# First products on x times its gain, with rstd applied to the results; pooling, head margins and adaptive-norm sums in another order

## The chip, the cores and the metric

One NeuronCore of a Trainium2 chip runs the whole program; nothing is shared with other cores. The metric is the device time of one execution in microseconds. Five engines work from queues of their own, each in order: TensorE (PE: products and transposes), VectorE (DVE), ScalarE (ACT), GpSimd (POOL) and SyncE (SP, which here only starts loads). They meet only through semaphores. POOL, ACT and SP can each start DMA loads; a load that must wait holds up everything behind it on the queue that starts it.

## The reference

256 tokens of width 2048 go through two transformer blocks. What matters here of the first is the norm, the first products and the two mixers:

```python
h = rms_norm(x, pre_mix_g)          # x * rstd * g, rstd one number per token
z = h @ w_in                        # q, k, v, u: 1024 columns each
a = chunked_attention(q, k, v, rel_bias)   # 8 heads of 128, chunks of 64 tokens
p = multiscale_pool(u, pool_w, pool_scale) # trailing means over 2, 4, 8, 16 tokens, minus the token
m = concatenate([a, p]) @ w_o
x = x + rms_norm(m, post_mix_g)
# then an FFN with gelu and a depthwise convolution over tokens, D_FF = 5632
```

The second block has adaptive norms: silu(c) @ w_ada + b_ada gives shifts, scales and gates for the token stream, and the same with c_ctx for a context of 256 tokens. w_ada has 2048 x 12288 numbers. The shift and scale of the first norm are needed before the second block's first product, the gates and the second norm's pair later. The block's k and v are computed for context and tokens together, then come 24 heads, gates, an output product and a second FFN.

## The kernel before

**Products.** All weights are float32. Every weight piece (128 x 1024, 512 KB) is loaded by SP into one of 4 buffers w, then split: ACT rounds it to h (L237, `prep`), DVE computes l = w - h (L238). Activations are kept as such a pair too. A product is h.h + l.h + h.l, so PE multiplies three times. There are 5 pairs of h and l; `fill`, called after each step of a product (`done`), prepares pieces as long as buffers allow, so ACT and DVE run some four pieces ahead of PE. `token_major` (L392, L393, L395) gives results with tokens on partitions: one block of 128 rows of weights is 6 matmuls of 512 columns for two token tiles, 12 for four. `feature_major` (L359) gives 128 features with 256 tokens on columns, in four steps of 8 matmuls; `folded` (L367 on ACT, L368 on DVE) adds its two halves and frees the bank.

**Order.** Code order is the order on every engine. `Side` holds generators of side work (pools, heads, norms of the second block): after each step of a product a `tick` advances one of them, or two in later stages, up to its next `yield n`, which lets n ticks pass. `side.until` ticks until a condition holds, with no product in between.

**Start.** SP loads x for the first 128 tokens, the gain row broadcast to all partitions (prg, 1 MB), four weight pieces, then x for the other tokens (L608, L610, L204). Per token tile: squares on ACT (L477), their sum and rsqrt (L426, L428 on DVE, a power on POOL, L429), x * rstd * g on DVE (L439), transposes on PE (L452), split into the pair (L337, L338). The first product, half of v, runs on 8 blocks for tile 0 alone, then makes tile 1, then goes on with both (`staged`). After it the conditioning rows are loaded (cc), passed through silu and written to DRAM (crow), to come back as broadcast rows (`ada_rows`, L510).

**After it.** vout splits v (L337, L338). DVE zeroes part of the probabilities' tiles by copying the zero margin of ut (L654), which POOL sets (L652) after another memset, on the table of position biases (tab, loaded as rb, L651). Then q and k are projected, heads 0 to 3 are added as side work, u is projected, and after every second feature block a `pool` is added: POOL adds shifted copies (L666), DVE scales and subtracts (L669 to L673), ACT and DVE split (L675, L676).

**Sums for w_ada.** Products with one row are done on DVE: tiles of w_ada come on POOL's queue into two buffers v (L211), one DVE instruction multiplies with the broadcast row and accumulates (L536). The first 64 tiles (shift and scale, both streams) take two sums each, every later tile one. `pace`, a number of sums per step from the table PACE (its first entry for feature_major, its second for token_major), spreads them over the products: entry 0 up to the first FFN, 1 in it, 2 in the second block's k and v, then two more. `limit` is the count of tiles allowed so far, `hold` the tick before which none may run. The rows for the sums and the gain of the last norm of block 1 (pfg) share one buffer, adat.

**Second block's k and v.** Six chunks of 512 columns for four token tiles (context and tokens). Seven banks hold results, so a chunk starts with three free banks and waits for the fourth: square on ACT (L1158), sums per head (L1159), power on POOL (L1161), scaling from the bank on DVE (L1190). Results go to DRAM on POOL's queue (L1196).

Of the kernel before, what the change touches and what calls it, by code (L numbers as in the profile page):

```python
# [20 lines left out]
F32 = mybir.dt.float32  # L21
# [14 lines left out]
PACE = ((0.3, 0.35), (0.19, 0.33), (0.0, 0.88), (0.0, 0.3), (0.1, 0.13))  # L36
# [154 lines left out]
class Stream:  # L191
# [10 lines left out]
    def load(self):  # L202
        while self.loaded < len(self.items) and self.loaded < self.mains + len(self.w):
            self.nc.sync.dma_start(self.w[self.loaded % len(self.w)], self.items[self.loaded])  # L204
            self.loaded += 1
# [65 lines left out]
class Kernel:  # L271
# [216 lines left out]
    def constants(self):  # L488
# [12 lines left out]
        self.small = self.g(P)  # L501
# [95 lines left out]
    def block1(self):  # L597
# [5 lines left out]
        xr = a["x"].rearrange("(t p) d -> p t d", p=P)  # L603
        nc.scalar.copy(self.stats[:, 0:1], self.mhalf)
        grow = self.slot(4, F32)[:, :D]
        for t in range(2):
            for c in range(4):
                nc.sync.dma_start(xt[:, t, c * 512:(c + 1) * 512], xr[:, t, c * 512:(c + 1) * 512])  # L608
            if t == 0:
                nc.sync.dma_start(grow, a["prg"].to_broadcast([P, D]))  # L610
                S.load()
        nc.scalar.dma_start(self.vecs, a["vec"])
        self.xs = self.ring(512, 4)

        def start(t):
            ss = self.stat(4)
            for c in range(4):
                self.sumsq(xt[:, t, c * 512:(c + 1) * 512], ss[:, c:c + 1])
            return self.pre_norm(t, xt, ss, grow)
        self.meet(self.norm_b(start(0), 0, hh, hl))  # L620
        xs1 = start(1)
        first = self.token_major([(hh, hl, 0), (hh, hl, 1)], self.staged(lambda: self.norm_t(xs1, 1, hh, hl)))
        cc = self.small[:32]
        nc.gpsimd.dma_start(cc, a["cc"])
        nc.scalar.activation(cc, cc, AF.Silu)
        nc.gpsimd.dma_start(self.crow.rearrange("o (j p) -> (o j) p", p=P), cc)
        self.pace = PACE[0]
        self.ada_begin({0: 0, 1: 2}, 64)
# [8 lines left out]
        scr = [s6[:, 2048 + i * 384:2048 + (i + 1) * 384] for i in range(4)]  # L637
        self.gtop = self.gbase + 1024 + 2048
# [9 lines left out]
        self.half = half  # L648
        nc.gpsimd.dma_start(tab, a["rb"])
        nc.gpsimd.dma_start(inv, a["inv"])  # L650
        nc.gpsimd.memset(tab[0:64, :, 192:256], NEG)  # L651
        nc.gpsimd.memset(ut[:, :, :16], 0.0)  # L652
        for i in range(4):
            nc.vector.tensor_copy(pt[:, i % 2, i // 2, 1, :P], ut[:, :8, :16])  # L654

        def pool(g):

            w = 2 ** (g + 1)
# [3 lines left out]
            while step < w:  # L662
# [4 lines left out]
                cur, step = dst, 2 * step  # L667
            fix = self.stat(32).rearrange("p (k t) -> p k t", k=2)
# [49 lines left out]
        def head(h):  # L718
# [10 lines left out]
            sc = 1.0 / math.sqrt(P)  # L729
            mx, sm = self.stat(2), self.stat(2)  # L730
            for q, (lo, hi) in enumerate(((0, P), (P, 384))):
                nc.vector.scalar_tensor_tensor(s[:, lo:hi], bank[:, 2 * lo:2 * lo + hi - lo], sc, tab[:, h, P:] if q == 0 else tab[:, h, :],
# [33 lines left out]
        vout(first)  # L766
        qkproj(0)
# [148 lines left out]
    def ffn1(self, pair, x, mid):  # L916
# [58 lines left out]
        def chunk_end(gi, c, t, bank):  # L975
# [11 lines left out]
            if gi == len(GROUPS) - 2 and c == 3 and t == 1:  # L987
                side.drain()
                S.finish()
# [590 lines left out]
```

## Time and profile before

| | |
|---|---|
| Median of 3 runs | 2774.2 us (2769.51 to 2774.95) |
| The profiled execution's own time | 2776.85 us |
| Its span, first to last instruction | 2775.1 us |
| Busy: PE, DVE, ACT, POOL | 97%, 73%, 48%, 9% |
| Mean granted clock of PE | 0.993 of 2.4 GHz |
| DMA | 608.91 MB, mean 219 GB/s |

PE is busy nearly all the time, so the shares say little on a change that leaves PE's work as it is. What PE waits for is read from the stages: 0 to 41 us is the start and the first product, 41 to about 320 the mixers of block 1, 320 to 368 the norms before the first FFN, 368 to 1058 that FFN, 1138 to 1404 the second block's k and v. The columns of a timeline row are start, duration, engine, line, operation, output and input, and in brackets the idle time before it and what ended it.

### The profile page before, as it was taken

To read this page: it belongs to the slowest core of one execution; us is meant where nothing else is said; L and a number is where in the kernel's file an instruction comes from. 1 tells how busy PE (TensorE), PEld (TensorE's weight loads), DVE (VectorE), ACT (ScalarE), POOL (GpSimd) and SP (SyncE) were. 2 spreads that over 40 slices of the span, in tenths; PEclk is the share of its full clock that TensorE was granted. 3 is DMA by queue.
4 is the path that set the end of the run, shared out by engine and by line. 5 is a ranking of instruction groups with operands and counts; after the bars stand their busy time and mean duration, and the time that the engine had idled before them with its cause. 6 is when DMAs were issued, how large, how long until landed. Compare 5 with 4: busy or idle time off the path is not lost.

```text
span 2775.1 us, 36806 instructions
## 1 busy us (share of the span) xinstructions
PE 2699.4 (97%) x13654; PEld 2274.2 (82%) x13654; DVE 2015.8 (73%) x2938; ACT 1336.8 (48%) x1994; POOL 248.8 (9%) x395
## 2 busy tenths in 40 slices
PE   7989899999999999998999999999999999999999
PEld 6878788888888887777777788888878888888887
DVE  5878787888887767767577877778766666665566
ACT  5444455545455645321256655644454444444443
POOL 1010000000000000222211100011000000000000
PEclk9999999999999999999999999999999999999999
DMA  7666667676776765666855544489857777766565
GB/s 264 199 217 230 241 211 259 220 251 215 244 238 207 227 191 168 232 245 243 292 178 178 171 155 156 148 322 322 274 170 227 236 230 233 234 198 195 185 205 166
DMA packets 167573, 608.91 MB, mean 219 GB/s; under 512 B 19472, under 2 KB 19664, under 8 KB 166368
## 3 DMA queue, kind: packets, MB, share of 16 engines
q1 hardware_dynamic: 127728, 461.43, 49.6%
q0 software_dynamic: 39520, 144.87, 15.8%
q8 instruction: 107, 1.75, 0.3%
q14 instruction: 74, 0.61, 0.1%
q10 hardware_dynamic: 144, 0.25, 0.0%
HBM read 591.76 MB, written 14.71 MB: 219 GB/s over the span
## 4 chain that ended last, share of the span: by engine, by line
PE 78%; DVE 3%; DMA 3%; ACT 2%; issue 2%; POOL 0%; DVEq 0%; ACTq 0%; POOLq 0%
PE bank L359 34%; PE bank L392 14%; PE bank L393 13%; PE bank L395 13%; DMA v<-wada 3%; PE bank L342 1%; DVE l L238 1%; PE bank L343 1%; PE bank L344 1%; PE bank L1275 1%; ACT h L237 1%; DMA G<-kv 0%; ACT G L477 0%; PE bank L452 0%; DVE G L536 0%
## 5 line engine op out<-in xcount | busy, mean ns | idle before, releaser
L238 DVE TENSOR_TENSOR l<-w,h 128x1024 fp32r<-128x1024 f32 x870 | 1059.9, 1225 | 357.6 <-ACT h L237 346.8
L237 ACT CAST h<-w 128x1024 fp32r<-128x1024 f32 x870 | 908.9, 1051 | 615.8 <-PE bank L393 430.9
L359 PE MATMUL bank<-pair,h 128*128 128x512 f32 x3072 | 842.8, 395 | 6.5 <-DVE slot L338 3.5
L359 PEld LDWEIGHTS bank<-pair,h 128*128 128x128 f32 x3072 | 526.7, 189 | 76.4 <-issue 3.7
L392 PE MATMUL bank<-h,pair 128*128 128x512 f32 x1344 | 539.3, 401 | 24.1 <-DVE slot L1190 10.3
L393 PE MATMUL bank<-h,pair 128*128 128x512 f32 x1344 | 530.0, 394 | 2.1 <-DVE G L426 1.4
L359 PEld LDWEIGHTS bank<-pair,l 128*128 128x128 f32 x3072 | 470.1, 189 | 66.6 <-DVE l L238 0.8
L359 PE MATMUL bank<-pair,l 128*128 128x256 f32 x3072 | 488.1, 281 | 0.1
L395 PE MATMUL bank<-l,pair 128*128 128x512 f32 x1344 | 416.0, 395 | 6.0 <-DVE l L238 5.9
L536 DVE CUSTOM_DVE_ANT_0 G<-v,G 128x1024 bf16<-128x1024 f32 x256 | 327.8, 1280 | 70.5 <-DMA v<-wada 68.8
L392 PEld LDWEIGHTS bank<-h,pair 128*128 128x128 f32 x1344 | 256.5, 191 | 83.5 <-issue 16.3
L395 PEld LDWEIGHTS bank<-l,pair 128*128 128x128 f32 x1344 | 255.3, 190 | 64.0 <-DVE l L238 9.5
L393 PEld LDWEIGHTS bank<-h,pair 128*128 128x128 f32 x1344 | 256.3, 191 | 53.6 <-DVE G L426 1.8
L392 PE MATMUL bank<-h,slot 128*128 128x512 f32 x768 | 299.1, 390 | 1.0 <-ACT slot L337 1.0
L393 PE MATMUL bank<-h,slot 128*128 128x512 f32 x768 | 299.0, 389 | 0.0
L395 PE MATMUL bank<-l,slot 128*128 128x512 f32 x768 | 237.7, 389 | 0.0
L211 POOL DMA_DIRECT2D v<-wada x192 | 102.1, 532 | 1337.7 <-DVE G L536 1281.0
L367 ACT COPY G<-bank 128x256 f32<-128x256 f32 x192 | 71.6, 373 | 278.5 <-PE bank L359 278.2
L392 PEld LDWEIGHTS bank<-h,slot 128*128 128x128 f32 x768 | 144.2, 188 | 30.8 <-ACT slot L337 1.5
L393 PEld LDWEIGHTS bank<-h,slot 128*128 128x128 f32 x768 | 144.2, 188 | 30.4 <-DVE slot L338 0.5
L395 PEld LDWEIGHTS bank<-l,slot 128*128 128x128 f32 x768 | 144.1, 188 | 30.0
L368 DVE TENSOR_TENSOR G<-bank,G 128x256 f32<-128x256 f32 x192 | 81.1, 422 | 109.4 <-ACT G L367 109.1
(217 smaller groups left out, 1700.4 us busy)
## 6 DMA issues: line engine op xcount, KB each, us to landing
v<-wada POOLq DMA_DIRECT2D x192, 512.0 KB, 4.8
w<-wup SPq DMA_DIRECT2D x176, 512.0 KB, 4.3
w<-wgu SPq DMA_DIRECT2D x176, 512.0 KB, 4.0
w<-wdn SPq DMA_DIRECT2D x88, 512.0 KB, 4.5
w<-wfd SPq DMA_DIRECT2D x88, 512.0 KB, 4.1
w<-w SPq DMA_DIRECT2D x66, 512.0 KB, 4.5
w<-w2g SPq DMA_DIRECT2D x64, 512.0 KB, 3.5
w<-w2kv SPq DMA_DIRECT2D x52, 512.0 KB, 4.4
```

What stands on the lines that cost most here:

```text
L211: self.nc.gpsimd.dma_start(t, src)
L237: self.nc.scalar.copy(h, w)
L238: self.nc.vector.tensor_sub(l, w, h.bitcast(F32))
L342: t.matmul(out, ah, bh, start=start, stop=False)
L343: t.matmul(out, ah, bl, start=False, stop=False)
L359: t.matmul(bank[:, :size], w[:, j * P:(j + 1) * P], x[:, kb, :size], start=s == n == 0, stop=s == 3 and n == 7)
L367: self.nc.scalar.copy(z, bank[:, 256:])
L368: self.nc.vector.tensor_add(out, bank[:, :256], z)
L392: self.nc.tensor.matmul(banks[i], xh, h, start=seen[i] == 1, stop=False)
L393: self.nc.tensor.matmul(banks[i], xl, h, start=False, stop=False)
L395: self.nc.tensor.matmul(banks[i], xh, l, start=False, stop=seen[i] == total[i])
L536: nc.vector.tensor_tensor_reduce(out=self.junk.bitcast(mybir.dt.bfloat16), in0=w, in1=self.adat[:, slot * 1024:(slot + 1) * 1024], scale=1 ...
```

## The change

The first norm is taken apart. x is multiplied by g alone, in chunks of 512 columns, transposed and split; rstd comes later and is applied to the product's results: to v while it is split (L809, L810 of the new kernel), to u and k by an extra DVE multiplication with a row rt of rstd per token (L741, L731), to q through the heads' scale (rq in place of the constant). The row rt goes through DRAM: two writes of 128 numbers (rrow) and one broadcast load. x and the gain are loaded chunk by chunk on three queues, with weight pieces between them on SP. The first product does one block, then chunk 1 is made, four blocks, chunk 2, four blocks, chunk 3, and the rest. Silu, crow and the table's memset become side work (`side_rows`). A pool starts after the one before and yields between POOL's adds and DVE's part. The sums get other paces, and when the first 64 tiles are done in the first FFN, 24 tiles more are allowed there, before the second block.

```diff
-PACE = ((0.3, 0.35), (0.19, 0.33), (0.0, 0.88), (0.0, 0.3), (0.1, 0.13))
+PACE = ((0.2, 0.3), (0.24, 0.36), None, (0.0, 0.3), (0.1, 0.13))
...
+        if kind == 0:
+            self.ada_begin({0: 0, 1: 1}, 88)
...
+        for c in range(4):
+            (nc.scalar if c == 0 else nc.gpsimd).dma_start(grow[:, cs[c]], a["prg"][:, cs[c]].to_broadcast([P, 512]))
+            nc.sync.dma_start(xt[:, 0, cs[c]], xr[:, 0, cs[c]])
+            if c < 2:
+                S.load(2 * c + 1)
+            (nc.scalar if c == 0 else nc.gpsimd).dma_start(xt[:, 1, cs[c]], xr[:, 1, cs[c]])
+            if c < 2:
+                S.load(2 * c + 2)
...
+        def scaled(c, t):
+            z, bank = xs(), self.sb()
+            nc.vector.tensor_mul(z, xt[:, t, cs[c]], grow[:, cs[c]])
+            for j in range(4):
+                nc.tensor.transpose(bank[:, j * P:(j + 1) * P], z[:, j * P:(j + 1) * P], self.ident)
+            return bank
...
+        first = self.token_major([(hh, hl, 0), (hh, hl, 1)], [
+            self.seg(range(1), after=lambda: chunk(1)), self.seg(range(1, 5), after=lambda: chunk(2)),
+            self.seg(range(5, 9), after=lambda: chunk(3)), self.seg(range(9, KB))])
+        for c in (2, 3):
+            squares(c)
+        rrow = self.dpool.tile([1, 256], F32, name="rrow")
+        for t in range(2):
+            self.rstd(ss[t], D, rr[:, t:t + 1], count=4)
+            nc.gpsimd.dma_start(rrow[:, t * P:(t + 1) * P].rearrange("o p -> p o"), rr[:, t:t + 1])
+        nc.vector.tensor_scalar_mul(rq, rr, 1.0 / math.sqrt(P))
...
+        nc.gpsimd.dma_start(rt, rrow.to_broadcast([P, 256]))
...
+        nc.gpsimd.memset(ut[:, :, :16], 0.0)
         nc.gpsimd.dma_start(tab, a["rb"])
         nc.gpsimd.dma_start(inv, a["inv"])
-        nc.gpsimd.memset(tab[0:64, :, 192:256], NEG)
-        nc.gpsimd.memset(ut[:, :, :16], 0.0)
...
         def pool(g):
 
+            while g and g - 1 not in pool_done:
+                yield 1
...
+            yield 2 + g
             fix = self.stat(32).rearrange("p (k t) -> p k t", k=2)
...
-                self.folded(self.feature_major(hx), ut[:, fb, 16:])
+                u = self.folded(self.feature_major(hx), ut[:, fb, 16:])
+                nc.vector.tensor_mul(u, u, rt)
...
+                    if which:
+                        nc.vector.tensor_mul(last, last, rt)
...
-                self.split(vt[:, 0, t, :], vt[:, 1, t, :], banks[t])
+                v, r = vt[:, 0, t, :], rr[:, t:t + 1]
+                nc.scalar.activation(v, banks[t], AF.Identity, scale=r)
+                nc.vector.scalar_tensor_tensor(vt[:, 1, t, :], banks[t], r, v.bitcast(F32), op0=ALU.mult, op1=ALU.subtract)
...
-                self.pace = PACE[2]
+                self.pace = 0.0, (132 - S.vdone) / 80
```

On DVE at the very start, the old kernel begins with the statistics of the first token tile (G) and goes over to pairs of l and pair:

```order
L426 TENSOR_REDUCE G<-G 128x1
L428 TENSOR_SCALAR G<-G 128x1
L439 SCALAR_TENSOR_TENSOR G<-slot_104,G,slot_107 128x512 x4
L238 TENSOR_TENSOR l_87<-w_78,h_82 128x1024
L338 TENSOR_TENSOR pair_105<-bank_75,pair_105 128x4x128
L238 TENSOR_TENSOR l_88<-w_79,h_83 128x1024
```

The new one begins with two multiplications of chunk 0 (slot_104 is x, slot_106 the gain):

```order
L625 TENSOR_TENSOR G<-slot_104,slot_106 128x512 x2
L239 TENSOR_TENSOR l_87<-w_78,h_82 128x1024
L339 TENSOR_TENSOR pair_105<-bank_75,pair_105 128x4x128
L239 TENSOR_TENSOR l_88<-w_79,h_83 128x1024
L339 TENSOR_TENSOR pair_105<-bank_76,pair_105 128x4x128
L239 TENSOR_TENSOR l_89<-w_80,h_84 128x1024
L239 TENSOR_TENSOR l_90<-w_81,h_85 128x1024
L625 TENSOR_TENSOR G<-slot_104,slot_106 128x512 x2
```

The statistics are gone from there, and the multiplications of chunk 1 stand behind the l of the fourth piece. On POOL, the old kernel has between the first rsqrt and the first w_ada tile (v):

```order
L429 TENSOR_TENSOR G<-G 128x1 x2
L624 DMA G<-cc 32x128
L626 DMA crow<-G 32x128
L510 DMA G<-crow 128x1024 x2
L649 DMA slot_332<-rb 128x2048
L650 DMA G<-inv 128x64
L651 MEMSET slot_332 64x8x64
L652 MEMSET G 128x8x16
```

and the new one, after six loads of x and the gain:

```order
L430 TENSOR_TENSOR G<-G 128x1
L654 DMA rrow<-G 128x1
L430 TENSOR_TENSOR G<-G 128x1
L654 DMA rrow<-G 128x1
L666 DMA slot_334<-rrow 128x256
L678 MEMSET G 128x8x16
L679 DMA slot_334<-rb 128x2048
L680 DMA G<-inv 128x64
L687 DMA G<-cc 32x128
L690 DMA crow<-G 32x128
L511 DMA G<-crow 128x1024 x2
L693 MEMSET slot_334 64x8x64
```

The zero margin (128x8x16) moved ahead of rb and behind rrow. In the norm of the context, which runs in the first FFN, POOL before has only the context's loads:

```order
L872 DMA G<-ctx 128x512 x4
L429 TENSOR_TENSOR G<-G 128x1
L879 DMA G<-ctx 128x512 x4
```

and now, at the same place:

```order
L920 DMA G<-ctx 128x512
L212 DMA v_93<-wada 128x1024
L430 TENSOR_TENSOR G<-G 128x1
L927 DMA G<-ctx 128x512
L212 DMA v_92<-wada 128x1024
L212 DMA v_93<-wada 128x1024
L212 DMA v_92<-wada 128x1024
L927 DMA G<-ctx 128x512
```

Tiles of w_ada now stand between them. Counted over DVE's list, the sums before the first FFN go from 55 to 41, those in it from 73 to 111, those in the second block's k and v from 64 to 40, and the later ones are 64 as before. Of those in the FFN, 24 stand between the fourth group's down product and the fifth group's up product, where before had none. PE has the same 8841 rows in both.

## Rows read from the trace of the kernel before

**Rows 1.** The page's busy line.
```profile
PE 2699.4 (97%) x13654; PEld 2274.2 (82%) x13654; DVE 2015.8 (73%) x2938; ACT 1336.8 (48%) x1994; POOL 248.8 (9%) x395
```
**Rows 2.** Stretches: from:to us, length, PE busy (count), PE clock, DMA share, GB/s.
```profile
0.00:41.00 41.00, 28.84 (x131) 1.00 0.76 275
41.00:62.00 21.00, 17.55 (x92) 0.92 0.65 237
...
130.00:172.00 42.00, 32.59 (x149) 0.92 0.43 137
...
368.00:1058.00 690.00, 690.00 (x3673) 1.00 0.69 226
...
1225.00:1264.00 39.00, 36.86 (x156) 0.96 0.57 207
1264.00:1302.00 38.00, 30.51 (x124) 0.87 0.61 220
```
**Rows 3.** Timeline of the start: us, duration, engine, line, operation.
```profile
9.94 2.74 DVE L439 SCALAR_TENSOR_TENSOR G<-slot,G,slot 128x512 f32<-128x512 f32 x4 [1.16 <-DMA slot<-prg]
...
11.11 1.05 ACT L237 CAST h<-w 128x1024 fp32r<-128x1024 f32 x1 [2.70 <-DMA w<-w]
...
12.60 1.22 DVE L238 TENSOR_TENSOR l<-w,h 128x1024 fp32r<-128x1024 f32 x1
...
21.68 2.64 PE L452 MATMUL bank<-G 128*128 128x128 f32 x16 [1.39 <-DVE G L439]
...
24.08 0.48 PE L392 MATMUL bank<-h,pair 128*128 128x512 f32 x1
...
40.50 1.07 ACT L337 CAST slot<-bank 128x512 fp32r<-128x512 f32 x2 [0.27 <-PE bank L395]
```
**Rows 4.** Start's stretches, all engines (PE, PEld, DVE, ACT, POOL); GB/s last.
```profile
0.00:8.00 8.00, 0.00 (x0) 0.00 (x0) 0.00 (x0) 3.95 (x9) 0.79 (x8) 1.00 0.72 244
8.00:16.00 8.00, 5.25 (x24) 4.86 (x25) 6.37 (x10) 5.30 (x9) 0.57 (x1) 1.00 1.02 406
```
**Rows 5.** Timeline around the first q projection.
```profile
53.26 0.52 POOL L651 MEMSET slot<- 64x512 f32 x1 [6.48 <-DMA slot<-rb]
...
53.95 0.63 DVE L654 CAST slot<-G 128x128 fp32r<-128x128 f32 x4 [14.09 <-POOL G L652]
...
55.33 2.04 PE L359 MATMUL bank<-pair,h 128*128 128x512 f32 x4 [3.45 <-DVE slot L338]
```
**Rows 6.** DMA issues from 39 to 56: KB each, us to landing.
```profile
crow<-G POOLq DMA_DIRECT2D x1, 16.0 KB, 3.8
```
**Rows 7.** Timeline around the third pool.
```profile
145.17 4.31 POOL L666 TENSOR_TENSOR G<-G 128x542 f32<-128x542 f32 x3 [4.76 <-DVE G L368]
...
149.51 0.19 DVE L669 TENSOR_TENSOR G<-G 128x32 f32<-128x32 f32 x1 [3.29 <-POOL G L666]
...
151.46 1.99 ACT L237 CAST h<-w 128x1024 fp32r<-128x1024 f32 x2
...
152.55 0.80 PE L392 MATMUL bank<-h,pair 128*128 128x512 f32 x1 [5.65 <-ACT h L237]
```
**Rows 8.** Page, costliest groups: multiplication-like DVE work on 256 columns.
```profile
L368 DVE TENSOR_TENSOR G<-bank,G 128x256 f32<-128x256 f32 x192 | 81.1, 422 | 109.4 <-ACT G L367 109.1
```
**Rows 9.** Page, costliest groups: the sums for w_ada.
```profile
L536 DVE CUSTOM_DVE_ANT_0 G<-v,G 128x1024 bf16<-128x1024 f32 x256 | 327.8, 1280 | 70.5 <-DMA v<-wada 68.8
```
**Rows 10.** DVE's waits from 1138 to 1380: total us, times, longest.
```profile
DVE G L536 <- DMA v<-wada: 64.0, 45, 3.6
```
**Rows 11.** PE's waits from 1374 to 1404.
```profile
PE bank L1264 <- DMA G<-kv: 3.8, 1, 3.8
PE bank L561 <- DVE G L536: 1.6, 1, 1.6
```
**Rows 12.** DVE busy in two stretches of the first FFN.
```profile
836.00:880.00 44.00, 31.06 (x43) 1.00 0.69 222
880.00:972.00 92.00, 69.78 (x115) 1.00 0.67 217
```

More of the change, by code (lines that the diff above doesn't have):

```diff
@@ L200, in __init__, with load @@
         self.pace, self.credit, self.limit, self.hold = 0.0, 0.0, 0, 0
-    def load(self):
-        while self.loaded < len(self.items) and self.loaded < self.mains + len(self.w):
+    def load(self, most=None):
+        most = len(self.items) if most is None else most
+        while self.loaded < most and self.loaded < self.mains + len(self.w):
             self.nc.sync.dma_start(self.w[self.loaded % len(self.w)], self.items[self.loaded])
@@ L500, in constants @@
         self.junk = self.g(512)
-        self.small = self.g(P)
+        self.small, self.rx = self.g(P), self.g(4)
         make_identity(nc, self.ident)
@@ L615, in start @@
[L615 to L625, printed above, removed]
@@ L626, in block1 @@
-        nc.gpsimd.dma_start(self.crow.rearrange("o (j p) -> (o j) p", p=P), cc)
-        self.pace = PACE[0]
-        self.ada_begin({0: 0, 1: 2}, 64)
+        grow = self.slot(4, F32)[:, :D]
+        cs = [slice(c * 512, (c + 1) * 512) for c in range(4)]
+        for c in range(4):
[6 more added lines that the diff above has]
+                S.load(2 * c + 2)
@@ new lines, in block1 @@
+        nc.scalar.dma_start(self.vecs, a["vec"])
+        nc.scalar.copy(self.stats[:, 0:1], self.mhalf)
+        xs = self.ring(512, 4)
+        ss = [self.ss[:, :4], self.ss[:, 4:]]
+        rq, rr = self.rx[:, :2], self.rx[:, 2:]
+        def scaled(c, t):
[4 more added lines that the diff above has]
+            return bank
@@ new lines, in parts, with chunk, squares @@
+        def parts(c, t, bank):
+            self.split(*(d[:, 4 * c:4 * c + 4, t * P:(t + 1) * P] for d in (hh, hl)), bank.rearrange("p (k t) -> p k t", k=4))
+        def chunk(c):
+            for t, bank in enumerate([scaled(c, 0), scaled(c, 1)]):
+                parts(c, t, bank)
+            if c > 1:
+                squares(c - 2)
+        def squares(c):
+            for t in range(2):
+                self.sumsq(xt[:, t, cs[c]], ss[t][:, c:c + 1])
+        begin = scaled(0, 0), scaled(0, 1)
@@ new lines, in block1 @@
+        for t in range(2):
+            S.prep()
+            parts(0, t, begin[t])
+        first = self.token_major([(hh, hl, 0), (hh, hl, 1)], [
[4 more added lines that the diff above has]
+        rrow = self.dpool.tile([1, 256], F32, name="rrow")
+        for t in range(2):
+            self.rstd(ss[t], D, rr[:, t:t + 1], count=4)
+            nc.gpsimd.dma_start(rrow[:, t * P:(t + 1) * P].rearrange("o p -> p o"), rr[:, t:t + 1])
@@ L648, in block1, with side_rows @@
         self.half = half
+        nc.gpsimd.memset(ut[:, :, :16], 0.0)
         nc.gpsimd.dma_start(tab, a["rb"])
         nc.gpsimd.dma_start(inv, a["inv"])
[L651 to L652 removed]
         for i in range(4):
             nc.vector.tensor_copy(pt[:, i % 2, i // 2, 1, :P], ut[:, :8, :16])
+        def side_rows():
+            cc = self.small[:32]
+            nc.gpsimd.dma_start(cc, a["cc"])
+            yield 6
+            nc.scalar.activation(cc, cc, AF.Silu)
+            nc.gpsimd.dma_start(self.crow.rearrange("o (j p) -> (o j) p", p=P), cc)
+            self.pace = PACE[0]
+            self.ada_begin({0: 0, 1: 2}, 64)
+            nc.gpsimd.memset(tab[0:64, :, 192:256], NEG)
+            yield 1
         def pool(g):
+            while g and g - 1 not in pool_done:
+                yield 1
             w = 2 ** (g + 1)
@@ L988, in chunk_end @@
                 side.drain()
+                S.limit = 64
                 S.finish()
                 side.drain()
-                assert S.vdone == 64 and len(self.ada_done) == 8
+                S.limit = S.vdone
+                assert len(self.ada_done) == 8
                 for n in range(4):
```

13 lines of the change are left out of this document (3 added, 10 removed).

## The prediction

> **What bounds the kernel now.** I read the page's busy line first: TensorE (PE) is busy 97% of the span [rows 1]. Then the table of stretches for PE [rows 2], cut where the program changes. The reader is to see two things there: from 368 to 1058 us (the first FFN) PE has no idle time at all, and what it loses elsewhere lies in a few short stretches. I count a stretch's loss as its length minus PE's busy time, plus its length times (1 - granted clock), since each of the lower figures comes from pieces at 1.2 instead of 2.4 GHz. That gives 12.2 us for 0 to 41; 3.5 + 1.7 = 5.1 for 41 to 62; 9.4 + 3.4 = 12.8 for 130 to 172; 2.1 + 1.6 = 3.7 for 1225 to 1264; 7.5 + 4.9 = 12.4 for 1264 to 1302. The order lists hold the same 8841 rows on PE in both kernels, so PE's own work is unchanged and the change can only give or take waits and clock. The rest is therefore: which wait of PE ends later or sooner, taken by stretch from the timelines and from the list of who waited for whom.
>
> **Start, 0 to 41 us.** Before, the first product ends at 40.50, when ScalarE (ACT) reads its bank; its last 72 matmuls start at 24.08, so one takes 0.228 us [rows 3]. The change splits x * g into chunks, and PE does one block of 6 matmuls, then the transposes of chunk 1, then the rest. On VectorE (DVE) the two multiplications of chunk 1 stand behind all of the first four l subtractions (the order list shows it), so they wait for the fourth weight piece. By then 4 pieces, 4 chunks of x and 2 of the gain must have come, 3.67 MB; with vec and all else on the ACT and POOL queues it is 4.97 MB. At the rates before, 244 and then 406 GB/s [rows 4], this is there at 12.2 or 15.4 us. Then come a cast of 1.05, a subtraction of 1.22, two multiplications of 0.69 (2.74 for 4 of their nearest kind) and a group of transposes of 0.66 (2.64 for 4 groups) [rows 3]: 4.3 us. PE then has 90 matmuls, 20.5 us, and 4 groups of transposes, 2.6 us. The product ends between 39.6 and 42.8, so -0.9 to +2.3 us. PE is idle for some 3 us in the middle of this. After waits of 3.5 and 5.7 us the clock fell [rows 2, 5, 7], and the shorter of these cost 1.7 us; that makes the upper end +4. I take +3, nearer that end, because three queues send at once and nothing puts the four pieces first. The statistics and the wait for the rsqrt, which stood ahead of the multiplication, go; but DVE was held there by the gain's load anyway, and the weights are late next.
>
> No row before shows three queues loading together. The Trainium skill, "DMA: Bandwidth & Descriptors", section "Issuing engines are not separate DMA queues", says that loads issued on several engines run on the same 16 DMA engines and interleave, and that spreading them saves only issue time. By that rule the later chunks on POOL delay the pieces, and the start is at or above the upper end just given; with full precedence for the pieces it would be at the lower.
>
> **First q projection, 41 to 62.** PE waited 3.5 us for DVE, whose copies (L654) waited for a POOL memset that stood behind another memset, which waited for the 1024 KB load of rb until 53.26 [rows 5]. Now the memset of the margin stands ahead of that load, but behind the two writes of rrow and the load that waits for them. A 16 KB write of this kind took 3.8 us [rows 6]; with some 4 us (an estimate) for the last squares, two reductions, two powers and two issues ahead of it, the memset runs about 8 us after the product ends. PE first missed DVE at 55.33 - 3.5 = 51.8, 11.3 us after the product's end. Two copies' and subtractions' time lies between, so about 1 us is left and the stall goes: -5.1, or -1 if the element-wise rrow write takes 4 us more. I take -5.
>
> **Pools and heads, 62 to 320.** In 130 to 172 PE's longest wait (5.7 us) ends with an ACT cast of weights at 151.46; ahead of that cast on ACT stands the pool's cast, which waits for DVE, which waits for three POOL adds of 4.3 us together [rows 7]. So a side task blocked two in-order queues that feed PE. Now each pool waits for the one before and lets 2 to 5 ticks pass between its adds and DVE's part; a tick has about 1.4 us of PE work behind it (four matmuls of 0.228 and four of half the columns), so 2.7 to 6.8 us. The largest pool has four adds of about 1.4 us, 5.7 us, just inside its 6.8. All of it would be -12.8; if POOL's adds are late behind a w_ada load, which itself waits for a sum on DVE, perhaps -5. I take -11. The 16 added multiplications by rstd cost 16 x 0.42 = 6.7 us of DVE [rows 8], and 14 fewer sums before the FFN give back 14 x 1.28 = 17.9 [rows 9]; neither is on PE's path, as DVE has idle time there. vout, the heads' scale and the other replaced operations keep their kind and size: nothing.
>
> **Second block's k and v, 1138 to 1404.** DVE waited 64.0 us here for w_ada tiles, 45 times [rows 10]: with two buffers the sums run as fast as loads land, and DVE falls behind the weights. In the fourth chunk, PE then waits 7.5 us for the evacuation; in the third, with the same instructions, only 2.1 [rows 2]. The change leaves 40 sums instead of 64, at 44/80 = 0.55 per block instead of 0.88, so the fourth chunk should cost what the third costs: 12.4 - 3.7 = -8.7. The floor is 0, if the wait is the chain's own. At the end PE waited 1.6 us for the last sum and 3.8 for kv [rows 11]; the last sums now come with slack, and the kv stores no longer stand behind the gate row: -2, between 0 and -5.
>
> **First FFN, 368 to 1058.** The sums moved there are not free. By the order lists 24 of them fall between the fourth group's down product and the fifth group's up product (836 to 972), where before had none. DVE is busy 31.06 of 44 and 69.78 of 92 there [rows 12]; 24 x 1.28 = 30.7 makes it 131.5 of 136. The ctx loads now also stand between w_ada loads on POOL. PE's cover is the weight pieces prepared ahead (four, some 11 us of PE work). Between 0 and +12; I take +4. Elsewhere in this FFN 14 more sums are spread over 470 us, where PE never waited: nothing.
>
> **Sum.** +3 - 5 - 11 - 8.7 - 2 + 4 = -19.7. The profiled execution took 2776.85 us (span 2775.1), so 2757.15; the median shown, 2774.2, lies 2.65 below it, which gives 2754.5.
>
> **Rivals.**
> - *The start loses more.* The later chunks take their full share, the pieces come at the end of the 4.97 MB, landing adds about 1 us and two pieces of low clock cost 3.4: +6.7 instead of +3, 2758.2. For it: the multiplications stand behind the fourth piece. Against: the SP queue alone holds the weights, in larger rows than x. This is where the skill's rule above would put the time. Chance 0.17.
> - *The pools' wait only moves.* POOL's adds still wait for DVE through the w_ada loads between them, DVE still waits for POOL: -1 instead of -11, 2764.5. For it: POOL's list still has such loads between adds. Against: the yields. Chance 0.1.
> - *The change doesn't do what it says at the k and v chunks*: the 7.5 us are the square, reduction and power in a row, not the sums: 2763.2. Against: the third chunk has the same chain and waits 2.1. Chance 0.1.
> - *The first FFN becomes bound by DVE*, the slower side. If from 836 on each of the 24 sums also waits for its tile as in [rows 10] (64.0/45 = 1.4 us), DVE needs 131.5 + 34 = 165.5 for 136, and with the in-order waits for ACT that its busy time doesn't hold, some 15 us (an estimate), 180. PE loses what exceeds 136 + 11 = 147: 33 instead of 4, 2784. It decides from the point where DVE's need passes 147. Against: at 0.24 and 0.36 per block (1.4 us of PE) the sums come every 4 to 6 us there, and in the k and v chunks before every 3.1 (0.88 per 2.7 us). Chance 0.05.
> - *My forecast*: 0.55, with a range of its own of 2746 to 2761. The remaining 0.03 is better than it: all terms at their lower ends, 2740.
>
> The range 2744 to 2768 holds the forecast and the first three rivals and leaves out the slower one and the best ends. About 0.2% (5.5 us) is what a measurement of this kernel can tell from no change: slower than before + 0.2% is the FFN rival, less the part of it that comes out milder, 0.04; within 0.2% (above 2768.7) that part and two small rivals together, 0.06; faster 0.90.
>
> **What would show it.** Right: the first product ends near 43 us; PE's wait of 3.5 near 52 and of 5.7 near 147 are gone, and the clock's low pieces with them; DVE's waits for wada in the k and v chunks fall from 64 to under 15 us; the fourth chunk's wait is near 2. Wrong: DVE waits for POOL of more than 3 us before the FFN, an L359 or L392 wait on an l subtraction between 836 and 1058, or a product that ends after 46.

## The result: 46 us slower

The changed kernel takes 2820.95 us (median; 2819.85 to 2822.52), the kernel before beside it 2774.57: a ratio of 1.017 with a 95% interval of 1.0153 to 1.0188. The forecast was 2754.5 us. The profiled execution has a span of 2819.4 us. Its busy line answers [rows 1]: PE is busy 19 us longer with the same instructions, at a mean granted clock of 0.987 in place of 0.993.

```profile
PE 2718.8 (96%) x13654; PEld 2285.7 (81%) x13654; DVE 2022.4 (72%) x2955; ACT 1335.9 (47%) x1994; POOL 258.7 (9%) x406
```

To see where the time went, I lined up PE's 12480 matmuls of weight pieces, which come in the same order in every kernel from the second product on, and read how much later than in the kernel before each one starts. Late by, in us, at points that are named by the time in the kernel before (the last columns are behind k and v, and the last matmul):

```
            46    102   139   358   751   1054  1561  2770
after       5.1   4.2  11.6  -2.9   3.3   57.2  45.0  44.1
e1          6.7   5.2  14.1   0.1   6.3    6.4   1.1  -0.6
e2          4.9   4.7  12.0  -2.4   4.9   17.1   2.7   1.3
e3          5.3   5.2  12.7   0.5   6.9   48.9  34.6  33.4
e4         -0.1  -1.5  -1.5  -1.5  -1.5   45.0  30.0  30.0
e5          6.0   6.0  10.8   6.8  11.9   19.6  14.7  14.7
e6          0.0   0.3   0.3  -7.0  -7.0   -7.0  -7.4  -8.8
e7          1.4   1.2   8.1  -4.4   2.1    2.2  -6.4  -6.9
e8          5.6   5.4  13.6   0.9   7.4   10.5  -1.2  -1.7
e9          1.3   2.9   8.1  -5.3   2.2    2.3  -4.9  -6.3
e10         0.0  -0.4  -0.4  -7.8  -7.9   -6.8 -20.2 -20.2
e11         1.3   1.1   7.6  -6.5  -5.1    1.8  -1.6  -1.5
e12         6.4   5.1  14.2   0.3   7.9    9.1  -5.9  -5.6
e13         1.4   1.0   6.7  -7.5  -1.4   -1.3  -9.2  -9.2
e14         1.4  -3.7   5.2  -9.9  -2.2    0.6 -12.9 -14.0
e15         1.5  -3.6   5.6  -6.6   0.0    3.4  -9.9 -10.9
e16         1.4  -3.0   3.2 -12.9  -6.4   -2.4 -14.1 -15.4
e17         1.5  -3.2   5.9  -6.5   0.0    3.5  -9.4 -10.1
```

Each line is one execution, the profiled one; where the code is the same (46 us in after, e1, e2, e3, e5, e8, e12), they spread from 4.9 to 6.7. That of e2 is the fastest of its eight executions (2778.33 us, median 2783.0), that of e14 the fastest of its ten. In the first line one stretch decides: between 839 and 938 us the changed kernel loses 54.3 us. The stretches that answer [rows 2] show the rest (from:to, length, PE, PEld, DVE, ACT and POOL busy, clock, DMA share, GB/s):

```profile
41.00:62.00 21.00, 18.77 (x97) 15.61 (x96) 8.53 (x18) 9.80 (x17) 4.56 (x9) 0.97 0.51 135
130.00:172.00 42.00, 42.00 (x228) 36.27 (x228) 38.84 (x58) 17.60 (x27) 16.79 (x12) 1.00 0.59 196
820.00:1062.00 242.00, 207.51 (x990) 174.41 (x989) 163.72 (x252) 106.18 (x171) 23.61 (x44) 0.90 0.66 223
1308.00:1346.00 38.00, 35.86 (x152) 29.20 (x151) 25.39 (x42) 8.26 (x10) 12.08 (x14) 0.96 0.56 200
```

The pools' stretch has no idle time left, and the fourth chunk of k and v has become like the third was. But in 820 to 1062, where PE never stopped before, it is idle for 34.5 us and loses 242 x 0.10 = 24.2 us by the clock, which after its waits falls to 1.2 GHz for pieces of the stretch (0.90 in the mean). The two overlap: their sum, 58.7, is a little more than the 54.3 lost. DVE is busy in only 164 of the 242 us there. The waits between 790 and 1010 us (who waited for whom: us in total, times, longest):

```profile
POOL v L212 <- DVE G L537: 145.0, 24, 13.3
ACT G L478 <- DMA G<-ctx: 43.8, 6, 8.2
DVE l L239 <- ACT h L238: 28.8, 20, 8.3
PE bank L360 <- ACT h L238: 15.0, 3, 6.0
DVE G L929 <- DMA G<-ctx: 12.3, 4, 5.0
PE bank L453 <- DVE G L929: 10.9, 4, 4.1
```

The kernel before, 800 to 1010 us:

```profile
POOL v L211 <- DVE G L536: 28.8, 2, 14.5
ACT G L477 <- DMA G<-ctx: 2.0, 2, 1.8
DVE G L881 <- DMA G<-ctx: 0.8, 2, 0.6
```

ACT and DVE wait 56 us for ctx where they waited 3. The timeline of the changed kernel shows how:

```profile
926.08 1.28 DVE L537 CUSTOM_DVE_ANT_0 G<-v,G 128x1024 bf16<-128x1024 f32 x1
...
930.29 0.54 POOL L212 DMA_DIRECT2D v<-wada  x1 [13.22 <-issue]
930.82 0.54 POOL L920 DMA_DIRECT2D G<-ctx  x1
935.86 0.63 ACT L478 ACTIVATE G<-G 128x512 f32<-128x512 f32 x1 [7.97 <-DMA G<-ctx]
936.49 1.03 ACT L238 CAST h<-w 128x1024 fp32r<-128x1024 f32 x1
937.55 1.23 DVE L239 TENSOR_TENSOR l<-w,h 128x1024 fp32r<-128x1024 f32 x1 [8.34 <-ACT h L238]
939.61 1.28 DVE L537 CUSTOM_DVE_ANT_0 G<-v,G 128x1024 bf16<-128x1024 f32 x1
941.19 0.53 POOL L212 DMA_DIRECT2D v<-wada  x1 [9.82 <-DVE G L537]
941.71 0.54 POOL L920 DMA_DIRECT2D G<-ctx  x1
946.71 0.63 ACT L478 ACTIVATE G<-G 128x512 f32<-128x512 f32 x1 [7.76 <-DMA G<-ctx]
```

Read it as a ring. A sum on DVE frees one of the two w_ada buffers; only then can POOL issue the next w_ada load, and the ctx load behind it. The ctx chunk lands 5 us later; ACT, whose next instruction squares it, has stood still, and the weight's cast behind the square with it; DVE waits for that cast, and behind it stands the next sum. A turn takes 11 us (930.82 to 941.71) and moves one chunk. (What ended POOL's wait before 930.29 the profile doesn't show; before 941.19 it was the sum.) The ctx loads also land more slowly than before, 5.5 us in place of 4.2 in the median, but over the ten waits that is some 13 of the 56 us (an estimate), and in e2 below, whose loads take 6.0 us, 9.6 us of the waits are left.

### The profile page after: what moved, and what is told of

It reads as the page before. It is cut to its first block, busy times and chain, and to the rows that moved or that the text cites. A ratio compares the mean times of both kernels' runs of the same rounds, so it can differ in the third digit from the quotient of the medians.

```text
span 2819.4 us, 36816 instructions
## 1 busy us (share of the span) xinstructions
PE 2718.8 (96%) x13654; PEld 2285.7 (81%) x13654; DVE 2022.4 (72%) x2955; ACT 1335.9 (47%) x1994; POOL 258.7 (9%) x406
## 4 chain that ended last, share of the span: by engine, by line
PE 73%; DVE 6%; issue 4%; ACT 2%; DMA 2%; POOL 1%; ACTq 0%; DVEq 0%; POOLq 0%
PE bank L360 28%; PE bank L393 14%; PE bank L394 14%; PE bank L396 14%; DVE l L239 2%; DMA G<-ctx 2%; ACT h L238 1%; DVE G L537 1%; PE bank L343 1%; PE bank L345 1%; PE bank L344 1%; PE bank L1325 1%; DMA G<-kv 0%; PE bank L453 0%; ACT G L478 0%
## 5 line engine op out<-in xcount | busy, mean ns | idle before, releaser
L360 PE MATMUL bank<-pair,h 128*128 128x512 f32 x3072 | 851.4, 398 | 16.7 <-ACT h L238 15.0
L393 PE MATMUL bank<-h,slot 128*128 128x512 f32 x768 | 302.9, 394 | 11.6 <-ACT slot L338 5.8
L393 PEld LDWEIGHTS bank<-h,pair 128*128 128x128 f32 x1344 | 254.6, 189 | 70.4 <-issue 10.9
L394 PE MATMUL bank<-h,slot 128*128 128x512 f32 x768 | 302.4, 394 | 2.1 <-DVE slot L339 2.1
L394 PEld LDWEIGHTS bank<-h,pair 128*128 128x128 f32 x1344 | 254.8, 190 | 54.3 <-DVE pair L339 5.1
```

The lines of the kernel that those rows point to most:

```text
L360: t.matmul(bank[:, :size], w[:, j * P:(j + 1) * P], x[:, kb, :size], start=s == n == 0, stop=s == 3 and n == 7)
L393: self.nc.tensor.matmul(banks[i], xh, h, start=seen[i] == 1, stop=False)
L394: self.nc.tensor.matmul(banks[i], xl, h, start=False, stop=False)
```

## Experiments

**The lost stretch.** Theory A is that ring; theory B is DVE's capacity, the forecast's slower rival. e1 is the changed kernel without the early start of the sums:

```
-        if kind == 0:
-            self.ada_begin({0: 0, 1: 1}, 88)
```


> The changed kernel without its early start of the 24 sums of the sh2 kind: all of them run beside the k/v products again. Against the changed kernel's 2821 us. Theory A (the POOL queue: in the first FFN the loads of ctx stand in POOL's order behind loads of w_ada, each of which waits for a sum on DVE, so ctx lands late and ACT and DVE wait for it with the weights' parts queued behind) and theory B (DVE's capacity: 24 x 1.28 us of sums are too much beside the FFN's own DVE work) both expect the 54 us that PE's products lose between 839 and 938 us of the kernel before's time to go, and 8 to 12 us of the k/v phase's waits for w_ada to come back: 2771 to 2779 us. Theory C (the stretch is lost to the new paces, the new limits of the first products or PE's clock, whatever the sums do) expects 2805 us or more.

2775.43 us, ratio to before 1.0006 (0.9996 to 1.0016): the 54 us are gone (6.3 late at 751, 6.4 at 1054). C falls.

e2 is the changed kernel with the ctx loads one chunk ahead (the loop that scales the chunks is changed in the same way; `load` issues what the two lines did):

```
+        ahead = [load(0, 0)]
+        yield 3
...
             for c in range(4):
-                z = self.rows()
-                nc.gpsimd.dma_start(z, cr[:, t, c * 512:(c + 1) * 512])
-                self.sumsq(z, ss[:, c:c + 1])
+                ahead.append(load((c + 1) % 4, t))
+                self.sumsq(ahead.pop(0), ss[:, c:c + 1])
```


> The changed kernel with all its sums where it has them, and each load of a ctx chunk given to POOL's queue one chunk earlier than its use (same queue, same two buffers, same number of loads). Theory A: the wait is the landing of a load that was issued too late; one chunk ahead hides most of it, so 35 to 54 of the 54 us go and the time is 2767 to 2786 us; ACT's waits for G<-ctx (43.8 us between 790 and 1010 us) fall under 10 us. Theory B: DVE has the same work as in the changed kernel, so 2812 us or more.

2783.0 us, 1.0033 (1.0022 to 1.0045). With the same loads, queue and sums the stretch (751 to 1054) costs 12.2 instead of 54 us in the profiled execution; by the medians of the whole kernel the edit gives back 38 us. POOL still waits 120 us for DVE (145 before the edit); it is ACT that no longer waits:

```profile
POOL v L212 <- DVE G L537: 120.4, 24, 10.8
ACT G L478 <- DMA G<-ctx: 9.6, 3, 5.6
```

The Trainium skill ("DMA: Bandwidth & Descriptors", "Rules for kernel authors") advises to issue a load early, compute, and wait late. The trace agrees: one chunk earlier gave back 42 us of the stretch.

e3 is the changed kernel with short sums:

```
+                wd = 128 if kind == 3 and n < 24 else 1024
...
-                    nc.vector.tensor_tensor_reduce(out=self.junk.bitcast(mybir.dt.bfloat16), in0=w,
+                    nc.vector.tensor_tensor_reduce(out=self.junk.bitcast(mybir.dt.bfloat16)[:, :wd], in0=w[:, :wd],
```


> The changed kernel with the first 24 sums of the sh2 kind over 128 columns instead of 1024 (it leaves out seven eighths of these 24 sums; the loads, their queue and their waits stay). DVE is relieved of about 24 x 1.0 = 24 us in the first FFN. Theory A: the loads still wait for each sum in DVE's order and ctx behind them, DVE was not full there (151.6 us busy of 220), so under a third of the 54 us goes: 2803 to 2822 us. Theory B: nearly all of it goes: 2763 to 2780 us.

2811.61 us, 1.0133 (1.0118 to 1.0148): 42 us stay lost with an eighth of the sums' work. B falls as the main cause.

```profile
POOL v L212 <- DVE G L539: 136.1, 24, 12.4
ACT G L478 <- DMA G<-ctx: 40.4, 6, 9.3
DVE G L931 <- DMA G<-ctx: 19.7, 5, 7.0
```

e4 is the kernel before with the early sums alone:

```
+        if kind == 0:
+            self.ada_begin({0: 0, 1: 1}, 88)
...
+                S.limit = 64
                 S.finish()
...
-                self.pace = PACE[2]
+                self.pace = 0.0, (132 - S.vdone) / 80
```


> The kernel before with one part of the change alone: the 24 sums started in the first FFN, with the limit's reset behind it and the pace of the k/v phase that follows from it. Theories A and B: about 54 us lost in the first FFN, 8 to 12 us gained in the k/v phase: 2812 to 2824 us. Theory C (the sums alone do not do it): 2760 to 2780 us.

2807.63 us, 1.0118 (1.0103 to 1.0134), 4 us under the expected range: this part alone loses 46.5 us in the first FFN and gains 15 in k and v. It is enough to turn the result.

e12 is e2 and e3 in one:

> The kernel of e2 (ctx loads a chunk ahead, 24 early sums) with e3's short sums: 24 sums over 128 columns instead of 1024 (seven eighths of them left out), the loads as they are. It asks what the 12 us are that e2 still loses in the first FFN. Theory D (they are DVE's own time, 24 x 1.1 us of sums in a stretch where DVE is busy 140 of 164 us): they go down to 3 us or less, 2771 to 2776 us; with e3 it then takes both edits to clear the stretch, the queue being 40 of the 54 us and DVE's work the rest. Theory A2 (they too are POOL's loads waiting for sums, since the ring has two buffers): 2779 us or more.

2772.0 us, 0.9992 (0.9982 to 1.0002). Of e2's 12 us one is left, and PE is idle for 0.8 us in 820 to 1062:

```profile
820.00:1062.00 242.00, 241.22 (x1275) 206.73 (x1274) 177.18 (x302) 134.18 (x209) 26.98 (x48) 1.00 0.77 266
```

So the 54 us are about 42 of late ctx loads, 11 of DVE's own work, and 1 that neither edit touches. By medians of the whole kernel the sizes are 38 to 40 (after to e2, e3 to e12) and 9 to 11 (after to e3, e2 to e12).

**The paces and the place at 448 us.** Here the changed kernel loses 6.0 us that the forecast did not have.

e5 is e1 with the old paces:

```
-PACE = ((0.2, 0.3), (0.24, 0.36), None, (0.0, 0.3), (0.1, 0.13))
+PACE = ((0.3, 0.35), (0.19, 0.33), None, (0.0, 0.3), (0.1, 0.13))
```


> The kernel of e1 (the changed kernel, its 24 sums back beside k/v) with the two paces of the sums that the kernel before had (0.3, 0.35 beside the first products and 0.19, 0.33 in the first FFN instead of 0.2, 0.3 and 0.24, 0.36). Theory P (the new FFN pace puts more sums between the last products of the first group; DVE's product of L1016 comes late and PE waits 3.8 us for its halves at 453 us): the 6.0 us that this place costs goes, the stretch of the heads (102 to 126 us) stays, 2768 to 2771 us. Theory Q (the wait belongs to where the sums stand after the new start, whatever the pace): 2773 to 2778 us.

2790.14 us, 1.0052 (1.0037 to 1.0067): both theories miss. The loss at 448 stays (4.9), and the old paces cost 6 us at 179 to 230, where e6 and e10 with the old paces lose 5 too, and 6 between 839 and 862. The new paces suit the new order better, by 14.7 us (2790.14 to 2775.43).

e11 is e7 (below) with the sums held at that place, in `ffn`:

```
+                if gi == 0 and n == 6:
+                    self.S.hold = max(self.S.hold, self.side.now + 16)
```


> The kernel of e7 with the sums held back for 16 steps at the end of the first group of the first FFN, where the kernel before happens to have none between 431 and 450 us. Theory H (what the changed kernel loses at 445 us is the two sums that now stand on DVE ahead of the last block's multiplication, not their pace, which e5 put back without effect): the 6.3 us of that place go, 2763 to 2766 us, less what the two sums cost later. Theory I (the last block's chain is late for another reason): 2769 to 2772 us.

2773.93 us, 0.9998 (0.9989 to 1.0008). PE's waits at 425 to 475 us, the changed kernel's first, then e11's:

```profile
PE bank L393 <- ACT slot L338: 3.7, 1, 3.7
```
```profile
PE bank L394 <- DVE slot L339: 0.5, 1, 0.5
```

The place is cured (1.2 us lost instead of 6.3), so theory H has the cause there; but 5.4 us come back at 839 to 862 and the gain in k and v is smaller (3.4 instead of 8.6), so that the time lies above both theories' ranges. Where the held sums go, a wait goes too.

**The pools.** e6 is the kernel before with the change's two edits to `pool`:

```
+            while g and g - 1 not in pool_done:
+                yield 1
...
                 cur, step = dst, 2 * step
+            yield 2 + g
```


> The kernel before with one part alone: the pools of the mixer one after the other, their DVE work some steps behind POOL's. Theory F (the forecast's term: 11 of the 12.8 us that PE waits for pools between 139 and 164 us go, nothing else moves): 2762 to 2766 us. Theory M (the pools' generators hold places among the four active ones, so the softmax of the first heads is pushed back, and the 7.4 us that the changed kernel loses at 102 to 126 us is the price): 2768 to 2774 us.

2766.93 us, 0.9971 (0.9959 to 0.9982), 0.9 us above theory F's range. The pools' stretch gains 12.4 us, as forecast, and 5.1 are lost again at 179 to 230. Theory M is wrong: the first heads are not late here (0.3 at 139).

**The start and the first heads.** e7 is e1 with chunk 1's multiplications ahead of the third and fourth l (`times` is the multiplication that stood in `scaled`):

```
             parts(0, t, begin[t])
+        early = {t: times(1, t) for t in range(2)}
...
-            z, bank = xs(), self.sb()
-            nc.vector.tensor_mul(z, xt[:, t, cs[c]], grow[:, cs[c]])
+            z, bank = early[t] if c == 1 else times(c, t), self.sb()
```


> The kernel of e1 with the two multiplications of chunk 1 put on DVE ahead of the third and fourth weight piece's l. Theory S (the start loses its 5 us because these two stand behind an l that waits for the fourth piece to land: PE waits 4.4 us for them at 20 us): PE's transposes of chunk 1 come at 15.6 us instead of 20, ACT's halves are then held by the cast of the fourth piece until 18, so about 3 us go: 2771 to 2774 us. Theory W (PE would wait for the third and fourth piece in any case, whose products come next): 2775 to 2777 us.

2770.09 us, 0.9982 (0.9973 to 0.9992). The start loses 1.4 instead of 6.7 us: theory S, and more than it asked. PE's transposes of chunk 1 start at 15.42 instead of 19.97:

```profile
15.42 1.91 PE L629 MATMUL bank<-G 128*128 128x128 f32 x8
```

e9 is e7 with the margin's memset ahead of rt's load:

```
-        nc.gpsimd.dma_start(rt, rrow.to_broadcast([P, 256]))
...
         nc.gpsimd.memset(ut[:, :, :16], 0.0)
+        nc.gpsimd.dma_start(rt, rrow.to_broadcast([P, 256]))
```


> The kernel of e7 (2770.1 us) with POOL's order turned at one place: the margin's memset ahead of the load of rt, which waits 7 us for rrow to land. Theory L (DVE stands behind that memset from 48 to 57 us with its l's; the weight loads behind them stop, DVE then runs late and the first heads come 4 to 7 us late at 102 to 120 us): DVE's copies come at 49 us, the q projection's stall of 3 to 4 us goes and a part of the heads' 6.8 us, 2760 to 2767 us. Theory N (the rest of the heads' loss is the new multiplications and the order of the side work, and the stall is ended by something else, such as the weights' landing): 2768 to 2771 us.

2771.5 us, 0.9987 (0.9978 to 0.9996). The stall at 55 us goes (1.3 late before it, 3.9 early behind it), and by 102 us it is back (2.9 late): ACT waits 13.8 us for the row cc. Behind the wait stood a second one.

e13 is e7 with the load of cc moved:

```
         nc.scalar.dma_start(self.vecs, a["vec"])
+        cc = self.small[:32]
+        nc.gpsimd.dma_start(cc, a["cc"])
...
-            cc = self.small[:32]
-            nc.gpsimd.dma_start(cc, a["cc"])
```


> The kernel of e7 with the load of the row cc at the front of POOL's queue (where x is loaded) instead of behind the table and rt; the Silu on it stays where it is. Theory K (ACT waits 13.6 us for cc before its Silu, the casts of the weight pieces stand behind, SP's weight loads stop from 52 to 60 us, DVE falls behind and with it k's parts and the first heads): ACT's wait goes, PE's stall at 60 us goes and a good part of the 6.8 us at 102 to 120 us: 2759 to 2766 us. Theory R (the heads' loss is DVE's twelve multiplications by rt and the margin's memset is the stall at 55 us): 2767 to 2771 us.

2769.73 us, 0.9983 (0.9974 to 0.9993). ACT's wait for cc is gone, PE's stall is not: it now ends with DVE behind the memset, as e9's ended with cc. Theory K fails; the time is in theory R's range.

e14 joins the edits of e7, e8, e9 and e13 on the changed kernel:

> The changed kernel with all repairs: chunk 1's multiplications early (e7), the margin's memset ahead of rt's load (e9), cc's load early (e13), ctx loads a chunk ahead and 12 early sums (e8). If the parts add: e8's 2773 us less 5 for the start, less 4 for the q projection and 0 to 7 for the heads, the 6 us at 445 us staying: 2757 to 2765 us. If the stalls give the time back to one another as e9's did: 2766 to 2770 us. e10's 2756 us is the mark to beat.

2768.98 us, 0.998 (0.9971 to 0.999). With both waits gone the q projection's 5 us stay gained (3.7 early at 102), but the first heads still lose 8.9 (5.2 late at 139). Its profiled execution is its fastest, 2763.2.

e15 is e14 with the loads of w_ada ahead of that of crow's rows:

```
+            self.S.vload()
             yield 6
```


> The kernel of e14 with the first two loads of w_ada issued by POOL ahead of the load of crow's rows instead of behind it. Theory V (DVE's wait of 6.2 us for the first of them puts k's parts and the first head's softmax late): the wait goes and 4 to 6 of the 9 us at 100 to 120 us: 2762 to 2766 us. Theory R (the heads are late by the multiplications by rt): 2767 to 2771 us.

2767.16 us, 0.9974 (0.9963 to 0.9984): inconclusive, since DVE then waits 5.4 us for crow's rows at the same place.

e16 is e14 without the multiplications by rt:

```
-                nc.vector.tensor_mul(u, u, rt)
...
-                    if which:
-                        nc.vector.tensor_mul(last, last, rt)
```


> The kernel of e14 without the twelve multiplications by rt (it leaves out rstd on k and on the pools' inputs). Theory R: 12 x 0.42 = 5 us less on DVE, four of them on the path to the first head's scores: 4 to 9 us of the heads' loss go, 2760 to 2765 us. Theory V: DVE waits for w_ada all the same, 2767 to 2770 us.

2762.18 us, 0.9956 (0.9939 to 0.9973). The edit takes out all 16 multiplications, not twelve as the expectation says. The heads lose 6.2 instead of 8.9: the multiplications are a third of it, less than theory R's 4 to 9 us; the median falls by 6.8.

e17 is e14 with Silu and crow's write moved from `side_rows`:

```
+        nc.scalar.activation(cc, cc, AF.Silu)
+        nc.gpsimd.dma_start(self.crow.rearrange("o (j p) -> (o j) p", p=P), cc)
         for c in (2, 3):
             squares(c)
```


> The kernel of e14 with Silu and the write of crow put ahead of the last sums of squares. Theory V (DVE's wait of 5 to 7 us for the first sum's operands puts everything behind it late, the first head too): the wait falls under 2 us and 4 to 6 of the 9 us lost at 100 to 120 us go: 2761 to 2766 us. Theory Z (the heads are late by the order in which sums, softmax and weight parts stand on DVE, not by that wait): the heads' loss stays over 7 us: 2767 to 2771 us.

2766.75 us, 0.9973 (0.9962 to 0.9984). DVE's longest wait for the first sum is down to 2.6 us, the heads still lose 9.1: theory V falls. What PE waits for is seen in two pairs of lines, the first head's scores on PE and their softmax on DVE, the kernel before, then the changed one:

```profile
92.55 0.28 PE L344 MATMUL bank<-slot 128*128 128x256 f32 x1
92.87 0.29 DVE L732 SCALAR_TENSOR_TENSOR slot<-bank,slot 128x128 f32<-128x128 f32 x1 [0.32 <-PE bank L344]
```
```profile
96.72 0.28 PE L345 MATMUL bank<-slot 128*128 128x256 f32 x1
...
103.22 0.35 DVE L777 SCALAR_TENSOR_TENSOR slot<-bank,G,slot 128x128 f32<-128x128 f32 x1
```

DVE comes to the scores 6 us after PE has them, in place of at once. Why it is behind, beyond the multiplications, stays open.

**Which sums are worth moving.** e8 is e2 with a limit of 76 in place of 88, 12 early sums instead of 24:

> The kernel of e2 (ctx loads a chunk ahead) with 12 early sums instead of 24. Theory A with what e2 left (10.7 us lost in the first FFN, where DVE is then busy 140 of 164 us): half the sums cost half or less, 2 to 5 us, and the k/v phase, which needs fewer than 24 sums moved for its wait of c=3, keeps 8 to 12 us of its gain: 2766 to 2775 us. Rival (the first sums are the costly ones, since the ctx loads run in the first half): 2777 us or more.

2773.17 us, 0.9987 (0.9977 to 0.9996). The FFN loses 3.1 us behind 751 instead of 12.2, and k and v still gain 11.7.

e10 joins e4's edits with the limit of 76, e2's and e6's on the kernel before:

> The kernel before with three parts: the pools in sequence (e6), 12 early sums, and the ctx loads a chunk ahead (e8's two); the start, the products on x * g and the paces stay as they were. If the parts add: e6's 7 us gained by the end of the first FFN's first half, 3 lost with the 12 sums and ctx, 12 gained in the k/v phase, 2 of which e6 has: 2757 to 2763 us. If they do not (the k/v wait is the chain's own once something else is faster, or the old pace of 0.19 leaves the early sums no room): 2764 to 2772 us.

2756.38 us (2754.94 to 2756.7), 0.9929 (0.9911 to 0.9948): 18.6 us faster than before, the best version found; its parts add, and come out 0.6 us better than the range. Its fourth chunk waits 2.1 us:

```profile
PE bank L392 <- DVE slot L1204: 4.9, 3, 2.1
```

## Why the prediction was wrong

Each step from the first line of the table, in us:

| step | forecast | measured |
|---|---|---|
| start | +3 | +5.1 |
| first q projection | -5 | -0.9 |
| pools and heads | -11 | -7.1 |
| first FFN | +4 | +60.1 |
| k, v and the tail | -10.7 | -12.2 |
| behind them | 0 | -1.0 |
| sum | -19.7 | +44.1 |

**First FFN: the step that failed.** The prediction wrote "The ctx loads now also stand between w_ada loads on POOL" and then priced only DVE's time and PE's cover. What that sentence names was the cause, and it got no price. What was missing is the question who is next in ACT's order behind the load: the square reads the chunk at once, the casts of the weights stand behind the square, and POOL, which used to run ahead of DVE, was now held to DVE's pace. e2 shows that this is 42 of the 54 us (38 by medians), e4 that 46.5 us are lost with nothing else of the change. DVE's capacity, which the +4 was for, is 11 us (e12), inside the stated 0 to 12. The slower rival had the right place with the wrong mechanism and too small a size (33 us): the sums waited for w_ada there 1.1 us in all, in two waits, not 34 us. The sign that was given for it, a wait of PE on an l subtraction, did not come up: PE waited most for the cast h (15.0 us in all) and for the ctx norm (10.9). Its chance of 0.05 was too small for a queue that was named and not followed. The remaining 6.0 us are at 448: "spread over 470 us, where PE never waited: nothing". In the changed kernel's trace two sums (438.72 and 444.23 us) stand on DVE in front of the last block's multiplication (445.43), and e11, which holds them back, loses 1.2 there; a place without waits is not one without a limit.

**Start: right place, term a little small.** The product ends at 45.6 us, just inside the mark of 46, and 5.1 late is above the stated upper end of +4. DVE's multiplications did wait behind the fourth piece [rows 3], and that piece was cast at 17.01 where the sum had it landed at 12.2 or 15.4, so the first rival's condition came true in part:

```profile
16.48 1.22 DVE L239 TENSOR_TENSOR l<-w,h 128x1024 fp32r<-128x1024 f32 x1 [2.60 <-ACT h L238]
...
17.01 1.04 ACT L238 CAST h<-w 128x1024 fp32r<-128x1024 f32 x1 [0.56 <-DMA w<-w]
18.09 1.23 DVE L239 TENSOR_TENSOR l<-w,h 128x1024 fp32r<-128x1024 f32 x1 [0.38 <-ACT h L238]
19.23 1.28 DVE L625 TENSOR_TENSOR G<-slot,slot 128x512 f32<-128x512 f32 x2
19.97 1.97 PE L627 MATMUL bank<-G 128*128 128x128 f32 x8 [4.39 <-DVE G L625]
```

The sum also has one group of transposes too few: chunk 1 has two (the eight matmuls at 19.97), and with them five groups follow the first, not four (0.66 us). The Trainium skill's rule that the loads of all queues interleave agrees with the rates (228 and 397 GB/s in the first two stretches of 8 us, no more than in [rows 4]). But the order on DVE is what made PE wait for these bytes: e7 gets 5.3 us back by order alone.

**First q projection: the bound that was named and not taken.** "-1 if the element-wise rrow write takes 4 us more": POOL waited 7.1 us for rrow to land (16 KB took 3.8 in [rows 6]), and the memset came 11.3 us after the product's end, the very limit. DVE's wait for POOL, 8.57 us, is the first of the prediction's signs of being wrong. Answering [rows 5]:

```profile
56.41 0.54 POOL L666 DMA_DIRECT2D slot<-rrow  x1 [7.11 <-DMA rrow<-G]
56.94 0.23 POOL L678 MEMSET G<- 128x128 f32 x1
57.20 0.68 DVE L682 CAST slot<-G 128x128 fp32r<-128x128 f32 x4 [8.57 <-POOL G L678]
...
58.68 1.16 PE L360 MATMUL bank<-pair,h 128*128 128x512 f32 x4 [1.69 <-DVE slot L810]
```

And the prediction did not see cc's load, which the diff moves behind the table's on POOL; ACT stood still for it:

```profile
66.17 0.31 ACT L689 ACTIVATE G<-G 32x128 f32<-32x128 f32 x1 [12.12 <-DMA G<-cc]
```

**Pools and heads.** At the pools 13.2 us came back where 12.8 were counted, as forecast; 7.4 were lost at the first heads, where "DVE has idle time" was taken as an average: the multiplications by rt stand between k's products and the first scores (e16: a third of the loss).

**k and v: the number right, the mechanism in part.** DVE's waits for wada fell from 64.0 us [rows 10] to 13.1, and PE's from [rows 11]'s 3.8 for kv to 0.4:

```profile
DVE G L537 <- DMA v<-wada: 13.1, 10, 3.0
```
```profile
PE bank L393 <- DVE slot L1240: 4.9, 3, 2.1
PE bank L1314 <- DMA G<-kv: 0.4, 1, 0.4
```

e4 shows that moving the sums is enough: with it alone the fourth chunk's wait falls from 7.5 to 2.1 us, and it is 2.1 to 3.0 in every kernel with 40 or 52 sums there. But moving them is not needed. In e7 all 64 sums stand beside k and v, DVE waits for wada as long as before (1138 to 1380 us), and the fourth chunk waits 2.1 us all the same (1260 to 1302 us):

```profile
DVE G L537 <- DMA v<-wada: 62.5, 45, 5.3
PE bank L393 <- DVE slot L1243: 2.1, 1, 2.1
```

In the other kernels with 64 sums that wait is 2.7 to 5.9 us (e9 and e13 2.7, e1 3.1, e6 4.4, e11 5.2, e5 5.9). What sets it there is open, so a part of this term is luck as far as is known. The end of the stage does go by the count: PE waits 1.6 to 5.8 us for the last sum in every kernel with 64 sums, and not at all in those with fewer.

## What to carry to other kernels

When loads with a small ring of buffers are moved onto an in-order queue, the queue runs at the pace of whoever frees the buffers (here POOL waited 24 times for a sum on DVE, 145 us in all); every other load on that queue then lands as late as that, so ask for each what stands behind its reader. Where a load's reader is the next instruction of an engine that others wait for, issue the load one step ahead: that was 42 of 54 us here. A wait that is removed may hide a second one behind it (memset and cc): look for the next one on each of the engines before a gain is booked.

## What was not expected of the hardware

An element-wise write of 0.5 KB (rrow, from 128 partitions) took a median of 6.9 us to land, longer than the 16 KB of crow (3.8 us in [rows 6]). That its form is the cause is not shown: in e14, where crow's write is issued right behind the 1024 KB of rb, it took 9.9 us, and rrow 8.8. Loads of ctx took 5.5 us in the median (3.3 to 10.1) beside the w_ada loads, 4.2 without them.
